# Two more buffers for raw weights, output blocks split ahead, and a dense copy of V in a hybrid S5 and delta-rule layer

## The chip, the core and the metric

The kernel runs on one core of a Trainium2 chip. The metric is the time of one execution in device microseconds. TensorE (PE in the rows) multiplies; its weight loads (PEld) are shown apart. VectorE (DVE), ScalarE (ACT) and GpSimd (POOL) work on tiles in on-chip memory, and SyncE (SP) issues most of the transfers. Smaller is better.

## The reference

One layer of a streaming encoder: 512 tokens of 2048 channels, float32. Cut to what matters here:

```
h  = LN0(x) * (1 + scale_m) + shift_m
p  = h @ W_in                      -> u_ssm, q, k, v, z, beta, a, gate_ssm, gate_gdn
ys = S5 (64 groups x 16 channels, 64 states each) + GLU, then -> 2048
yg = gated DeltaNet (8 heads, chunks of 64), then -> 2048
m  = sigmoid(gate_ssm) * ys + sigmoid(gate_gdn) * yg
x  = LN1(alpha * x + gate_m * (m @ w_mix_out))
h  = LN0(x) * (1 + scale_f) + shift_f
x  = LN2(alpha * x + gate_f * SwiGLU(h))        # hidden size 5632, 44 tiles of 128
```

The scales, shifts and gates come from a small product of the conditioning vector (adaLN).

## The kernel before

**Weights.** Weights are float32 and TensorE multiplies in a reduced float32 type (fp32r), so each weight block is split in two halves. `Weights` does it for a list of blocks of 128x1024 that is planned beforehand in the order of use. SP loads a block of 512 KB into a buffer `raw` (NB = 3 buffers), ACT casts it to `whi`, DVE subtracts and gets `wlo`. A product of one 128-row slice is three matmuls: hi with the activation's hi, lo with it, hi with the activation's lo. `next` hands out the next block. `run_ahead` splits two blocks beyond the one in use. `poll` is asked after every product and issues the next raw load once the planner's clock has passed the last use of the buffer that the load will take.

**Order.** The program is written through a small planner, `Order`: each call of an engine is recorded with a modelled cost, and side lines of work (the S5 mixer, the delta rule, the layer norms) are generators that the planner resumes between the weight products. `yield X` in such a line means: go on when X is ready by the planner's clock. All engine calls have the one line L170, matmuls L211, transposes L216, so groups are told apart by the tiles' names.

**S5.** The 64 groups are done in eight batches (`s5_batch`). Each computes powers V (tile s_V, on GpSimd), transposes them into G, and multiplies them by C into a convolution kernel Kc: two halves of four matmuls in float32, one for each lag tau. The stationary operand of a matmul is a slice of V whose elements lie eight apart. A matmul of this kind leaves two records in the trace.

**End of the mixers.** `switch()` closes the mixers' buffer pools and opens the buffers of the second half. The product with w_mix_out (tiles pm, blocks raw<-in_w_mix_out_dram) follows the merge.

**FFN.** The 44 hidden tiles come in groups of 8, 8, 8, 8, 8 and 4. A tile takes two products (gate and value) and leaves gs, which is split into hi and lo. After a group its part of the output is added to x (`xa`). The last group is different: after its four tiles, 16 output products of 12 matmuls follow, for token tiles t=0 to 3 and in each for column quarters q=0 to 3, each with its residual add and the statistics of LN2. Their eight weight blocks (two for each q) are multiplied by the row gate_f before they are split. Of these, blocks 0 to 2 go through `next` and are split in the usual way, blocks 3 to 7 through `raw_next`: loaded, and scaled and split by the side line `last_parts` just before use. `ws.limit` keeps `run_ahead` from splitting these five.

Of the kernel before, what the change touches and what calls it, by code (L numbers as in the profile page):

```python
# [11 lines left out]
F32 = mybir.dt.float32  # L12
# [146 lines left out]
class Engine:  # L159
# [5 lines left out]
    def __getattr__(self, name):  # L165
        f = getattr(self.e, name)

        def call(*a, **kw):
            assert self.k != "p" or name != "scalar_tensor_tensor"
            r = f(*a, **kw)  # L170
            out = kw.get("out", a[0] if a else None)
            ins = [x for x in _aps(kw, a) if x is not out]
            k = self.k
            if name == "dma_start":
                self.o.run(k, 1.0 if k == "p" else 0.06, out, ins, 0.05 + out.nbytes() / 345e3)
                return r
            n = 1
            for d in out.shape[1:]:
                n *= d
            if name == "bn_stats":  # L180
                n = 512
            if k == "v":
                us = 0.2 + n * (0.00055 if name in ("tensor_scalar", "tensor_copy", "memset") else 0.00105)
            elif k == "a":
                us = 0.2 + n * 0.00086
            elif kw.get("op") is ALU.pow:
                us = 0.2 + 0.17 * n
            else:
                us = 0.2 + n * (0.0021 if name == "tensor_tensor" else 0.0030)
            self.o.run(k, us, out, ins)  # L190
            return r
        return call
# [198 lines left out]
def s5_batch(k, j, prm, d_col):  # L391
# [56 lines left out]
    for half in range(2):  # L448
        pg = k.psum("s5")
        for i in range(4):  # L450
            pe.transpose(pg[:, 128 * i:128 * i + 128], V[:, 4 * half + i].rearrange("p h s -> p (h s)"), k.c(C_ID))
        act.copy(G[:, 4 * half:4 * half + 4].rearrange("p t n -> p (t n)"), pg)
    Kc = k.sm5.tile([128, 15, 16], F32, name="s5Kc", tag="s5Kc")
    pool.memset(Kc[:, 0:7], 0.0)
    for half in range(2):
        pk = k.psum("s5")
        for i in range(4):
            tau = 4 * half + i
            pe.matmul(pk[:, 128 * i:128 * i + 128], lhsT=V[:, :, :, 7 - tau].rearrange("p g h -> p (g h)"),
                      rhs=cf[:, 0, :], start=True, stop=True)  # L460
        yield pk
        pk4 = pk.rearrange("p (t n) -> p t n", t=4)
        v.tensor_tensor(out=pk4, in0=pk4, in1=bc(k.c(C_BD).unsqueeze(1), [128, 4, 128]), op=M)
        v.tensor_reduce(out=Kc[:, 7 + 4 * half:11 + 4 * half], in_=pk.rearrange("p (t g h) -> p t h g", t=4, g=8),
                        axis=mybir.AxisListType.X, op=A)
# [459 lines left out]
NHALF = 8  # L925


GATES_BEFORE = (0, 1, 1, 1, 1, 1, 1, 1)
WB = 1024
NB = 3  # L930


class Weights:


    def __init__(self, k, pool):
        self.k, self.pool = k, pool
        self.specs, self.raw, self.parts, self.names = [], {}, {}, {}
        self.used = self.loaded = self.cut = 0
        self.limit = None  # L940

    def plan(self, src, kts, cols, scale=None):
# [3 lines left out]
    def load(self, upto):  # L946
        while self.loaded < min(upto, len(self.specs)):
            src, kts, cols, _ = self.specs[self.loaded]
            t = self.pool.tile([128, WB], F32, name="raw", tag="raw")
            self.k.sync.dma_start(out=t[:, 0:kts * cols].rearrange("p (k n) -> p k n", k=kts),  # L950
                                  in_=src.rearrange("(k p) n -> p k n", p=128))
            self.raw[self.loaded] = t
            self.names[self.loaded] = t.name
            self.loaded += 1

    def split(self, upto):
        while self.cut < min(upto, len(self.specs) if self.limit is None else self.limit):
            i = self.cut
            self.load(i + 1)
            _, kts, cols, scale = self.specs[i]  # L960
            n = kts * cols
            raw = self.raw.pop(i)
            if scale is not None:
                self.scaled(raw, kts, cols, scale)
            hi = self.pool.tile([128, WB], F32R, name="whi", tag="whi")
            lo = self.pool.tile([128, WB], F32R, name="wlo", tag="wlo")
            self.k.act.copy(hi[:, 0:n], raw[:, 0:n])
            self.k.v.tensor_tensor(out=lo[:, 0:n], in0=raw[:, 0:n], in1=hi[:, 0:n].bitcast(F32), op=S)
            self.parts[i] = tuple(t[:, 0:n].rearrange("p (k n) -> p k n", k=kts) for t in (hi, lo))
            self.cut += 1  # L970
# [28 lines left out]
    def poll(self):  # L999

        i = self.loaded
        if i < len(self.specs) and i < self.cut + NB:
            o = self.k.o
            if i < NB or o.last.get(self.names[i - NB], 0.0) <= o.clock:
                self.load(i + 1)


# [1 line left out]
def kernel(ctx, tc, x, c, w_ada, b_ada, w_in, lam_re, lam_im, log_dt, b_re, b_im, c_re, c_im,  # L1009
# [5 lines left out]
    k = Ctx()  # L1015
# [67 lines left out]
    for hf in range(2):  # L1083
        for q in range(4):
            for c0 in range(0, 16, 2):
                ws.plan(w_mix[0, 128 * c0:128 * c0 + 256, 512 * q:512 * q + 512], 2, 512)
    groups = [(j0, min(HG, NHT - j0)) for j0 in range(0, NHT, HG)]
    ffn_order = []
    for gi, (j0, ng) in enumerate(groups):
        nh = min(NHALF, ng) if gi == 0 else 0  # L1090
        ffn_order.append([(j, [hf]) for hf in range(2) for j in range(nh)] + [(j, [0, 1]) for j in range(nh, ng)])
        for j, _ in ffn_order[-1]:
            for base in (0, HID):
                plan1(f_in[0, :, base + 128 * (j0 + j):base + 128 * (j0 + j) + 128])
        for q in range(4):
            for c0 in range(0, ng, 2):
                r0 = 128 * (j0 + c0)
                ws.plan(f_out[0, r0:r0 + 256, 512 * q:512 * q + 512], 2, 512, q if gi == len(groups) - 1 else None)
    ws.limit = len(ws.specs) - 5


    cst = cpool.tile([128, 128], F32, name="cst")
# [381 lines left out]
    def switch():  # L1484

        o.drain(s5l)
        o.drain(gl)
        o.MARGIN = 0.4
        sps.close()
        gps.close()  # L1490
        per5s.close()
        bp = ctx.enter_context(pool_of(name="bp", bufs=32))
        q2 = ctx.enter_context(pool_of(name="q2", bufs=2))
        P2.extend((bp, q2))

        def operands():
            for dst, src in ((zs, k.dz), (ygs, k.dy)):
                r = load2(src[0])
                for j in range(8):
                    yield r  # L1500
                    nxt = load2(src[j + 1]) if j < 7 else None
                    hi, lo = bt(), bt()
                    if dst is zs:
                        act.copy(nat(hi), by_pos(r))
                        v.tensor_tensor(out=nat(lo), in0=by_pos(r), in1=nat(hi).bitcast(F32), op=S)
                    else:
                        split(hi, lo, r)
                    dst.append((hi, lo))
                    r = nxt
        k.ada_deep = True  # L1510
        o.add(operands())
        o.add(ada_rest())
# [252 lines left out]

    for gi, (j0, ng) in enumerate(groups):
        if gi == len(groups) - 1:
            k.gf_rows = [row_to(t2("ld"), drow[5], q) for q in range(2)]
        for j, hs in ffn_order[gi]:
            if 1 in hs and gi == 0 and j == 0:  # L1770
                o.drain(lnl)
            ffn_tile(gsp[j], hs)
        if gi == len(groups) - 1:
            break
        for q in range(4):
            pss = [k.psum("fo") for _ in range(4)]
            o.until(lambda: k.ada_done)
            gf = row_of(drow[5], q)
            for c0 in range(0, ng, 2):
                hi, lo = ws.next(2, 512)  # L1780
                for t in range(4):
                    prod(pss[t], gsp, t, c0, ng, [hi[:, i, :] for i in range(2)], [lo[:, i, :] for i in range(2)])
                    if c0 + 2 == ng:
                        scaled(t, q, pss[t], gf)


    k.gf_rows += [row_to(bt(F32), drow[5], q) for q in range(2, 4)]
    parts = []

    def last_parts():  # L1790
        for q in range(4):
            his, los = [], []
            if q > 1:
                yield k.gf_rows[q]
            for c0 in range(0, ng, 2):
                if 2 * q + c0 // 2 < 3:
                    hi, lo = ws.next(2, 512)
                    his += [hi[:, i, :] for i in range(2)]
                    los += [lo[:, i, :] for i in range(2)]
                    continue  # L1800
# [58 lines left out]
```

## Time and profile before

| | |
|---|---|
| median of 3 runs | 3115.47 us (3112.6 to 3117.87) |
| profiled execution | 3112.85 us, its span 3111.1 us |
| mean granted TensorE clock | 0.987 |
| PE busy | 97% of the span |
| PEld, DVE, ACT, POOL busy | 80%, 53%, 31%, 26% |
| instructions | 40284 |

The profiled execution's time is that of the whole launch, the span that of its instructions. Busy times are shares of the span over all stages, which differ; what one stage is limited by is seen in the stretches below.

### The profile page before, as it was taken

To read this page: it belongs to the slowest core of one execution; us is meant where nothing else is said; L and a number is where in the kernel's file an instruction comes from. 1 tells how busy PE (TensorE), PEld (TensorE's weight loads), DVE (VectorE), ACT (ScalarE), POOL (GpSimd) and SP (SyncE) were. 2 spreads that over 40 slices of the span, in tenths; PEclk is the share of its full clock that TensorE was granted. 3 is DMA by queue.
4 is the path that set the end of the run, shared out by engine and by line. 5 is a ranking of instruction groups with operands and counts; after the bars stand their busy time and mean duration, and the time that the engine had idled before them with its cause. 6 is when DMAs were issued, how large, how long until landed. Compare 5 with 4: busy or idle time off the path is not lost.

```text
span 3111.1 us, 40284 instructions
## 1 busy us (share of the span) xinstructions
PE 3005.1 (97%) x15953; PEld 2488.9 (80%) x15953; DVE 1650.4 (53%) x2217; ACT 954.8 (31%) x1378; POOL 810.8 (26%) x904
## 2 busy tenths in 40 slices
PE   5999999999999999999899999999999999999996
PEld 3677788888788888888779988888888888888885
DVE  6646666667754577756787543333333333333337
ACT  3333233323332444323355522221221222222121
POOL 2079365555621255200132011003002001200302
PEclk8999999999999999999999999999999999999998
DMA  9743343333333698756776643333333333333342
GB/s 339 263 133 109 97 114 106 100 101 105 95 114 111 211 313 272 243 188 227 256 250 181 178 144 109 95 96 114 95 95 106 105 95 101 109 95 96 110 131 86
DMA packets 508925, 458.14 MB, mean 147 GB/s; under 512 B 56144, under 2 KB 403632, under 8 KB 508736
## 3 DMA queue, kind: packets, MB, share of 16 engines
q1 hardware_dynamic: 485536, 390.03, 41.1%
q0 software_dynamic: 16000, 52.44, 5.2%
q10 hardware_dynamic: 7200, 13.10, 1.2%
q8 instruction: 125, 2.05, 0.3%
q14 instruction: 64, 0.52, 0.1%
HBM read 435.60 MB, written 19.89 MB: 146 GB/s over the span
## 4 chain that ended last, share of the span: by engine, by line
PE 66%; DVE 4%; DMA 3%; issue 2%; ACT 1%; POOL 1%; ACTq 0%; DVEq 0%; SPq 0%; POOLq 0%
PE pm L211 48%; PE px_fo L211 14%; DMA raw<-in_w_mix_out_dram 2%; PE px_gd L211 1%; DVE at L170 1%; DVE wlo L170 1%; ACT whi L170 1%; PE px_s L211 1%; DMA raw<-in_ffn_w_in_dram 1%; DVE aacc L170 0%; DVE st L170 0%; PE px_ada L211 0%; DVE pm L170 0%; DVE raw L170 0%; POOL g_T L170 0%
## 5 line engine op out<-in xcount | busy, mean ns | idle before, releaser
L211 PE MATMUL pm<-at,whi 128*128 128x512 f32 (+1 forms) x3744 | 1133.8, 386 | 0.1
L170 DVE TENSOR_TENSOR wlo<-raw,whi 128x1024 fp32r<-128x1024 f32 x541 | 690.1, 1277 | 819.7 <-ACT whi L170 816.6
L170 ACT CAST whi<-raw 128x1024 fp32r<-128x1024 f32 x541 | 567.2, 1050 | 1061.8 <-PE pm L211 461.4
L211 PEld LDWEIGHTS pm<-at,whi 128*128 128x128 f32 x3744 | 679.4, 189 | 129.4 <-issue 3.5
L211 PE MATMUL pm<-at,wlo 128*128 128x512 f32 (+1 forms) x1872 | 713.0, 381 | 0.0
L211 PE MATMUL pm<-bt,whi 128*128 128x512 f32 (+1 forms) x2464 | 679.7, 362 | 0.0
L211 PEld LDWEIGHTS pm<-bt,whi 128*128 128x128 f32 x2464 | 442.4, 189 | 71.3 <-ACT whi L170 0.5
L211 PE MATMUL pm<-bt,wlo 128*128 128x512 f32 (+1 forms) x1232 | 445.9, 362 | 1.7 <-DVE wlo L170 1.7
L211 PEld LDWEIGHTS pm<-at,wlo 128*128 128x128 f32 x1872 | 353.9, 189 | 68.4 <-DVE wlo L170 0.4
L170 POOL TENSOR_TENSOR at<-at,ld 128x512 f32<-128x512 f32 x80 | 120.4, 1531 | 1003.0 <-DVE ld L170 1003.0
L211 PE MATMUL px_fo<-whi,bt 128*128 128x512 f32 x960 | 298.8, 389 | 0.0
L211 PEld LDWEIGHTS pm<-bt,wlo 128*128 128x128 f32 x1232 | 232.8, 189 | 38.1 <-DVE wlo L170 2.3
L211 PEld LDWEIGHTS px_fo<-whi,bt 128*128 128x128 f32 x960 | 180.1, 188 | 37.4
L211 PE MATMUL px_fo<-wlo,bt 128*128 128x512 f32 x480 | 186.7, 389 | 0.0
L170 DVE SCALAR_TENSOR_TENSOR aacc<-w,ccol,aacc 128x512 f32<-128x512 f32 x180 | 154.4, 858 | 4.5 <-DMA w<-in_w_ada_dram 3.4
L211 PE MATMUL pm<-whi,bt 128*128 128x512 f32 x336 | 109.2, 396 | 8.0 <-DVE at L170 8.0
L211 PE MATMUL px_fo<-whi,at 128*128 128x512 f32 x336 | 108.1, 391 | 1.7 <-ACT whi L170 1.7
L211 PEld LDWEIGHTS px_fo<-wlo,bt 128*128 128x128 f32 x480 | 90.1, 188 | 18.8
L170 DVE SCALAR_TENSOR_TENSOR gs<-gg,pm 128x512 f32<-128x512 f32 x36 | 24.8, 688 | 142.1 <-ACT gg L170 142.1
L170 DVE TENSOR_TENSOR gs<-gs,pm 128x512 f32<-128x512 f32 x36 | 24.7, 687 | 119.6 <-PE pm L211 119.6
L211 PEld LDWEIGHTS pm<-whi,bt 128*128 128x128 f32 x336 | 63.9, 190 | 23.5 <-DVE at L170 10.2
L211 PEld LDWEIGHTS px_fo<-whi,at 128*128 128x128 f32 x336 | 63.5, 189 | 15.2 <-ACT whi L170 2.1
(421 smaller groups left out, 3190.3 us busy)
## 6 DMA issues: line engine op xcount, KB each, us to landing
raw<-in_ffn_w_in_dram SPq DMA_DIRECT2D x208, 512.0 KB
raw<-in_w_in_dram SPq DMA_DIRECT2D x146, 512.0 KB
raw<-in_ffn_w_out_dram SPq DMA_DIRECT2D x88, 512.0 KB
wad<-in_w_ada_dram SPq DMA_DIRECT2D x64, 512.0 KB
w<-in_w_ada_dram SPq DMA_DIRECT2D x128, 256.0 KB
raw<-in_w_mix_out_dram SPq DMA_DIRECT2D x64, 512.0 KB
w<-in_w_ada_dram POOLq DMA_DIRECT2D x96, 256.0 KB, 4.9
gg<-in_w_ada_dram POOLq DMA_DIRECT2D x32, 256.0 KB, 5.2
```

The costliest lines, as they stand in the source:

```text
L170: r = f(*a, **kw)
L211: r = self.e.matmul(out, **kw)
```

## The change

Three parts:

1. In `s5_batch`, ACT copies V into a dense tile Vs, one plane of 128x128 for each lag, and the eight matmuls of the kernel Kc take their stationary operand from there. The tile takes the buffer "K" that later holds another matrix of the batch. ACT's modelled cost for operands of more than three dimensions is raised.
2. From `switch()` on, two more raw buffers (pool "more") stand in a ring with the three of before: raw, more, raw, more, raw. `poll` may then load up to five blocks beyond the last one split.
3. Four of the last eight output blocks (q=0 and q=1) are planned earlier: two behind the last group's first tile and two behind its second. They are loaded there, scaled and split into buffers that are free by then (`kept`, `spare`). Of the four others, two go through `next` and two through `raw_next`, and `ws.limit` leaves the last two out instead of five.

```diff
@@ Engine: modelled cost on ACT
-                us = 0.2 + n * 0.00086
+                us = 0.2 + n * (0.00195 if len(out.shape) > 3 or (ins and len(ins[0].shape) > 3) else 0.00086)
@@ s5_batch
+    Vs = k.t5w("K")
+    act.copy(Vs.rearrange("p (s n) -> p s n", s=8), V.rearrange("p g h s -> p s (g h)"))
+    yield Vs
...
-            pe.matmul(pk[:, 128 * i:128 * i + 128], lhsT=V[:, :, :, 7 - tau].rearrange("p g h -> p (g h)"),
+            pe.matmul(pk[:, 128 * i:128 * i + 128], lhsT=Vs[:, 128 * (7 - tau):128 * (8 - tau)],
                       rhs=cf[:, 0, :], start=True, stop=True)
@@ constants
+EARLY = 4
+MORE = 2
@@ Weights.load
-            t = self.pool.tile([128, WB], F32, name="raw", tag="raw")
+            pool, tag = self.ring[0]
+            self.ring.append(self.ring.pop(0))
+            t = pool.tile([128, WB], F32, name="raw", tag=tag)
+            self.past[tag].append(t.name)
@@ Weights.split
+            if i in self.kept:
+                pairs = self.kept[i]()
+                for s, (hi, lo) in enumerate(pairs):
+                    r = raw[:, cols * s:cols * s + cols]
+                    self.k.act.copy(hi, r)
+                    self.k.v.tensor_tensor(out=lo, in0=r, in1=hi.bitcast(F32), op=S)
+                self.parts[i] = tuple(zip(*pairs))
+                self.cut += 1
+                continue
@@ Weights.poll
-        if i < len(self.specs) and i < self.cut + NB:
-            o = self.k.o
-            if i < NB or o.last.get(self.names[i - NB], 0.0) <= o.clock:
+        tag = self.ring[0][1]
+        n = MORE if tag == "more" else NB
+        if i < len(self.specs) and i < self.cut + (NB + MORE if len(self.ring) > 1 else NB):
+            o, past = self.k.o, self.past[tag]
+            if len(past) < n or o.last.get(past[-n], 0.0) <= o.clock:
                 self.load(i + 1)
@@ the list of blocks
+            if last and j < EARLY // 2:
+                kept += range(len(ws.specs), len(ws.specs) + 2)
+                plan_out(2, True)
+        plan_out(len(out_blocks), last)
-    ws.limit = len(ws.specs) - 5
+    ws.limit = len(ws.specs) - 2
@@ switch
+        more = ctx.enter_context(pool_of(name="more", bufs=MORE))
+        ws.ring = [(wpool, "raw"), (more, "more"), (wpool, "raw"), (more, "more"), (wpool, "raw")]
@@ the last group
+            spare = gsp[ng:] + [[adp.tile([128, 512], F32R, name="w1", tag="w1", bufs=4) for _ in range(2)] for _ in range(2)]
...
+            if gi == len(groups) - 1 and j < EARLY // 2:
+                early += [ws.next(2, 512) for _ in range(2)]
...
@@ last_parts
-                if 2 * q + c0 // 2 < 3:
+                n = 2 * q + c0 // 2
+                if n < EARLY:
+                    his += early[n][0]
+                    los += early[n][1]
+                    continue
+                if n < 6:
```

Where instructions stand now, at three places. On ACT in the first S5 batch (s_G is G, s_K the buffer of the copy of V, g_ the delta rule, go and dg_101 a gate on its way to DRAM, s_S the batch's states):

```order
 L170 COPY s_G<-px_s_2476 128x512
 L170 COPY s_G<-px_s_2482 128x512
+L170 COPY s_K<-s_V 128x1024
 L170 COPY g_MT<-px_gd 128x512
-L170 COPY s_S<-px_s_2571 64x256 x4
 L170 ACTIVATE go<-pm 128x512
 L170 DMA dg_101<-go 128x512
```

The copy of V stands between the copies of G and a copy of the delta rule, and the batch's states are copied later.

On ACT at the first two tiles of the last FFN group, before (whi<-raw are weight blocks, gg the gate's activation, at<-gs the cast of a finished tile):

```order
L170 CAST whi<-raw 128x1024 x18
L170 ACTIVATE gg<-pm 128x512
L170 CAST whi<-raw 128x1024 x2
L170 CAST at<-gs 128x512
L170 CAST whi<-raw 128x1024 x2
L170 ACTIVATE gg<-pm 128x512
```

And there now (bt, w and aacc are the buffers that keep the early output blocks):

```order
L170 CAST whi<-raw 128x1024 x18
L170 ACTIVATE gg<-pm 128x512
L170 CAST bt<-raw 128x512 x4
L170 CAST at<-gs 128x512
L170 CAST whi<-raw 128x1024 x4
L170 ACTIVATE gg<-pm 128x512
L170 CAST w_22922<-raw 128x512
L170 CAST w_22924<-raw 128x512
L170 CAST aacc<-raw 128x512
L170 CAST aacc_22928<-raw 128x512
L170 CAST at<-gs 128x512
L170 CAST whi<-raw 128x1024 x4
```

Where two casts of the next tile's weights stood ahead of the cast of the finished tile, four casts of early output blocks stand now, and the next tile's casts come behind.

On DVE at the first of the last output products, before (raw<-raw,bt scales a block, bt<-raw,bt are its two subtractions, at<-at,pm and at<-at,px_fo residual adds, st statistics):

```order
L170 TENSOR_TENSOR at<-at,pm 128x512
L170 BN_STATS st<-at 128x6
L170 TENSOR_TENSOR raw<-raw,bt 128x1024
L170 TENSOR_TENSOR bt<-raw,bt 128x512 x2
L170 TENSOR_TENSOR raw<-raw,bt 128x1024
L170 TENSOR_TENSOR bt<-raw,bt 128x512 x2
L170 TENSOR_TENSOR raw<-raw,bt 128x1024
L170 TENSOR_TENSOR bt<-raw,bt 128x512 x2
L170 TENSOR_TENSOR raw<-raw,bt 128x1024
L170 TENSOR_TENSOR bt<-raw,bt 128x512 x2
L170 TENSOR_TENSOR at<-at,px_fo 128x512
L170 BN_STATS st<-at 128x6
```

And there now:

```order
L170 TENSOR_TENSOR gs<-gs,pm 128x512
L170 TENSOR_TENSOR bt<-gs,bt 128x512
L170 TENSOR_TENSOR raw<-raw,bt 128x1024
L170 TENSOR_TENSOR bt<-raw,bt 128x512 x2
L170 TENSOR_TENSOR raw<-raw,bt 128x1024
L170 TENSOR_TENSOR bt<-raw,bt 128x512 x2
L170 TENSOR_TENSOR at<-at,pm 128x512
L170 BN_STATS st<-at 128x6
L170 TENSOR_TENSOR at<-at,px_fo 128x512
L170 BN_STATS st<-at 128x6
```

Two blocks are split between the last tile and the first residual add, and none between the residual adds.

## Rows read from the trace of the kernel before

**Rows 1.** The page, busy time, share of the span and instructions of each engine.

```profile
PE 3005.1 (97%) x15953; PEld 2488.9 (80%) x15953; DVE 1650.4 (53%) x2217; ACT 954.8 (31%) x1378; POOL 810.8 (26%) x904
```

**Rows 2.** Stretches: length, busy time by engine (records), TensorE's clock, DMA share, GB/s.

```profile
300.00:900.00 600.00, 577.43 (x4211) 484.12 (x4209) 400.44 (x703) 202.29 (x400) 309.61 (x289) 0.98 0.37 103
1400.00:1440.00 40.00, 40.00 (x178) 33.13 (x177) 25.57 (x30) 13.59 (x15) 0.00 (x0) 1.00 0.61 201
1440.00:1480.00 40.00, 39.70 (x172) 31.85 (x171) 27.84 (x35) 14.95 (x16) 3.24 (x6) 1.00 0.79 254
1480.00:1520.00 40.00, 34.81 (x143) 27.23 (x142) 25.57 (x30) 12.54 (x13) 3.77 (x7) 0.96 0.80 262
1520.00:1560.00 40.00, 36.92 (x149) 28.48 (x148) 33.95 (x49) 15.21 (x16) 12.53 (x16) 0.96 0.76 245
1560.00:1600.00 40.00, 35.15 (x157) 27.57 (x156) 33.63 (x47) 19.91 (x27) 14.73 (x14) 1.00 0.75 247
```

**Rows 3.** Time line of PE at the end: start, duration, first matmuls of t=0, 1, 2.

```profile
3037.03 0.39 PE L211 MATMUL pm<-whi,at 128*128 128x512 f32 x1
...
3060.43 0.39 PE L211 MATMUL pm<-whi,at 128*128 128x512 f32 x1
...
3071.31 0.39 PE L211 MATMUL pm<-whi,at 128*128 128x512 f32 x1
```

**Rows 4.** Groups by form, PE: count, busy us, mean ns, idle before.

```profile
L211 PE MATMUL px_s<-s5Cs,s_V 128*128 128x128 f32 x128 | 32.8, 404 | 0.0
...
L211 PE MATMUL px_gd<-g_k 128*128 128x128 f32 x64 | 8.4, 275 | 0.0
```

**Rows 5.** Groups by form, weight loads of the same matmuls.

```profile
L211 PEld LDWEIGHTS px_s<-s5Cs,s_V 128*128 128x128 f32 x128 | 31.7, 332 | 0.4
...
L211 PEld LDWEIGHTS px_gd<-g_k 128*128 128x128 f32 x64 | 8.2, 191 | 0.5
```

**Rows 6.** Groups by form, ACT: the copy that is already made in each batch.

```profile
L170 ACT COPY s_K<-s_R 128x1024 f32<-128x1024 f32 x8 | 17.6, 2198 | 0.0
```

**Rows 7.** The chain in 1440 to 1600: start, duration, what; three of nine loads.

```profile
1495.94 10.53 DMA raw<-in_w_mix_out_dram
...
1522.82 6.05 DMA raw<-in_w_mix_out_dram
...
1586.29 3.78 DMA raw<-in_w_mix_out_dram
```

**Rows 8.** Waits of PE and ACT in 1440 to 1600: total us, times, longest.

```profile
PE pm L211 <- DVE at L170: 8.0, 5, 2.5
...
ACT whi L170 <- DMA raw<-in_w_mix_out_dram: 56.9, 28, 8.9
```

**Rows 9.** Two stretches of 3.4 us beside a gap; columns as in rows 2.

```profile
1540.60:1544.00 3.40, 0.93 (x5) 0.43 (x4) 3.29 (x6) 1.76 (x2) 1.68 (x3) 1.00 0.96 324
1544.00:1547.40 3.40, 3.40 (x8) 2.72 (x9) 3.33 (x6) 0.47 (x1) 3.32 (x4) 0.50 0.51 178
```

**Rows 10.** Time line of DVE in the last products.

```profile
3053.42 1.22 DVE L170 TENSOR_TENSOR raw<-raw,bt 128x1024 f32<-128x1024 f32 x1
...
3059.65 0.68 DVE L170 TENSOR_TENSOR at<-at,px_fo 128x512 f32<-128x512 f32 x1
...
3095.58 0.68 DVE L170 TENSOR_TENSOR at<-at,px_fo 128x512 f32<-128x512 f32 x1
```

**Rows 11.** Time line of DVE and ACT at a tile's end in the last group.

```profile
3015.47 0.69 DVE L170 TENSOR_TENSOR gs<-gs,pm 128x512 f32<-128x512 f32 x1 [3.35 <-PE pm L211]
...
3016.72 1.05 ACT L170 CAST whi<-raw 128x1024 fp32r<-128x1024 f32 x1
...
3017.80 1.22 DVE L170 TENSOR_TENSOR wlo<-raw,whi 128x1024 fp32r<-128x1024 f32 x1 [0.26 <-ACT whi L170]
```

**Rows 12.** Two more stretches; columns as in rows 2.

```profile
2950.00:3037.00 87.00, 87.00 (x385) 72.07 (x384) 29.58 (x29) 20.46 (x23) 10.11 (x15) 1.00 0.45 130
3060.40:3093.20 32.80, 32.80 (x145) 26.84 (x143) 29.56 (x49) 4.57 (x6) 14.43 (x11) 1.00 0.20 72
```

More of the change, by code (lines that the diff above doesn't have):

```diff
@@ L937, in __init__ @@
         self.k, self.pool = k, pool
-        self.specs, self.raw, self.parts, self.names = [], {}, {}, {}
+        self.specs, self.raw, self.parts, self.kept = [], {}, {}, {}
         self.used = self.loaded = self.cut = 0
+        self.ring, self.past = [(pool, "raw")], {"raw": [], "more": []}
         self.limit = None
@@ L952, in load @@
             self.raw[self.loaded] = t
-            self.names[self.loaded] = t.name
             self.loaded += 1
@@ L1086 @@
                 ws.plan(w_mix[0, 128 * c0:128 * c0 + 256, 512 * q:512 * q + 512], 2, 512)
+    kept = []
     groups = [(j0, min(HG, NHT - j0)) for j0 in range(0, NHT, HG)]
@@ L1091, with plan_out @@
         ffn_order.append([(j, [hf]) for hf in range(2) for j in range(nh)] + [(j, [0, 1]) for j in range(nh, ng)])
+        out_blocks = [(q, c0) for q in range(4) for c0 in range(0, ng, 2)]
+        def plan_out(n, scale=None):
+            for q, c0 in itertools.islice(out_blocks, n):
+                r0 = 128 * (j0 + c0)
+                ws.plan(f_out[0, r0:r0 + 256, 512 * q:512 * q + 512], 2, 512, q if scale else None)
+            del out_blocks[:n]
+        last = gi == len(groups) - 1
         for j, _ in ffn_order[-1]:
@@ L1094 @@
                 plan1(f_in[0, :, base + 128 * (j0 + j):base + 128 * (j0 + j) + 128])
[L1095 to L1098, printed above, removed]
-    ws.limit = len(ws.specs) - 5
+            if last and j < EARLY // 2:
[3 more added lines that the diff above has]
+    ws.limit = len(ws.specs) - 2
     cst = cpool.tile([128, 128], F32, name="cst")
@@ L1767 @@
         if gi == len(groups) - 1:
-            k.gf_rows = [row_to(t2("ld"), drow[5], q) for q in range(2)]
+            q2 = P2[1]
+            k.gf_rows = [row_to(t, drow[5], q) for q, t in enumerate((t2("ld"), t2("ld"), t2("grow")))]
+            spare = gsp[ng:] + [[adp.tile([128, 512], F32R, name="w1", tag="w1", bufs=4) for _ in range(2)] for _ in range(2)]
+            spare += [[adp.tile([128, 512], F32R, name=n, tag=n, bufs=1) for n in ("aacc", "go")],
+                      [q2.tile([128, 512], F32R, name=n, tag=n, bufs=1) for n in ("aacc2", "keep")]]
+            for n, i in enumerate(kept):
+                ws.kept[i] = lambda n=n: spare[2 * n:2 * n + 2]
+            early = []
         for j, hs in ffn_order[gi]:
@@ L1784 @@
                         scaled(t, q, pss[t], gf)
-    k.gf_rows += [row_to(bt(F32), drow[5], q) for q in range(2, 4)]
+    k.gf_rows.append(row_to(bt(F32), drow[5], 3))
     parts = []
@@ L1792, in last_parts @@
             his, los = [], []
-            if q > 1:
-                yield k.gf_rows[q]
+            yield k.gf_rows[q]
             for c0 in range(0, ng, 2):
-                if 2 * q + c0 // 2 < 3:
+                n = 2 * q + c0 // 2
[4 more added lines that the diff above has]
+                if n < 6:
                     hi, lo = ws.next(2, 512)
```

## The prediction

> **What bounds the kernel now.** I read the page first, then stretches. TensorE is busy 97% of the span [rows 1], so a gain must shorten TensorE's own work or fill one of its few gaps. A busy TensorE is not a full one, so I counted matmul records in stretches of equal length instead of trusting the busy time. At full rate, in 1400 to 1440, TensorE finishes 178 records in 40 us, one per 0.225 us; in the four stretches of 40 us behind it, the product with the mixers' output weights, it finishes 172, 143, 149 and 157 [rows 2]. That product loses time although its busy column hardly falls. The other stretch I looked for is the S5 and delta-rule phase, 300 to 900: busy 577.43 of 600, so 22.6 us idle there [rows 2]. The third is the end, where the output products of four token tiles t=0 to 3 follow one another. Tile t=0 starts at 3037.03, t=1 at 3060.43, t=2 at 3071.31: 23.4 us for the first and 10.88 for the next, with the same 48 accumulations each [rows 3].
>
> Each of the three parts of the change falls on one of these places.
>
> **(a) The dense copy of V.** It removes nothing and replaces 64 strided stationary operands by dense ones, for eight ACT copies. Records in the view by form: 128 matmul records with a column of V as stationary operand take 32.8 us, in 16 groups (two per batch), so 2.05 us a group of eight records. The delta rule's products of the same shape and type, 128x128x128 float32 with a dense operand, take 8.4 us for 64, 1.05 us for eight [rows 4]. The only difference that the rows offer is the read of the stationary operand: its weight load takes 332 ns against 191 [rows 5]. So a group gets 1.0 us shorter, 16 in all.
>
> Here a page speaks against the change. The Trainium skill, "TensorE: Matmul & The Clock Gate", section "LDWEIGHTS (loading the stationary operand)", gives a load as columns divided by 1.2 GHz and says that only the columns matter; by it a dense operand would save nothing and the sum would lose these 16 us. The measured loads differ by 1.7 times at the same 128 columns, so the row decides here.
>
> The price is eight ACT copies with the same strided read. The same copy of another matrix in each batch, s_K<-s_R, takes 2198 ns [rows 6], so 17.6 us of ACT. ACT is busy 202.29 of 600 us there [rows 2]: at the low end this is hidden beside other work, at the high end each copy stands in front of what the K products need and all 17.6 is paid. Only a S5 batch waits for its own copy, and TensorE has weight products to run meanwhile, so I take 2. (a) = −16 + 2 = **−14**, bounds −17 and +1.6.
>
> **(b) Two more raw buffers.** They remove the rule that a load can only start when the third block before it is used up. In the four stretches, 4×178 = 712 records would have been done at full rate; 172+143+149+157 = 621 were. The 91 missing are worth 91×0.225 = 20.5 us. How fast must a transfer be? A block is 12 matmuls, 12×0.225 = 2.7 us. With three buffers a buffer comes round every 8.1 us, of which the cast takes 1.05 and the subtraction 1.22 [rows 11], so 5.8 us are left for the load. With five it is 13.5 − 2.3 = 11.2. The chain of that stretch holds nine pieces of these loads, from 3.78 to 10.53 us, the middle one 6.05 [rows 7]. So half the pieces are too slow for three buffers, and all fit five. ACT's casts waited 56.9 us for these loads [rows 8]. The mean of the DMA engines is 0.75 to 0.80 busy [rows 2], so there is a reserve in rate, but not a big one: loads that start earlier compete with operands' loads. TensorE also waited 8.0 us for DVE, which draining products holds up [rows 8]; that the buffers do not mend. Part of the lost time is the clock: after a gap (TensorE busy 0.93 of 3.4 us) the next 3.4 us ran at 0.50, the lower level (1.2 GHz), with 8 records in place of 15 [rows 9]; without the gap this is not paid. I take three quarters of 20.5: **−15**, bounds −6 (the waits for DVE stay, and the gaps move) and −21 (all).
>
> A page would say that the loads were fast enough before. The Trainium skill, "DMA: Bandwidth & Descriptors", section "Anatomy of one DMA — SWDGE (gpsimd) path", fits a transfer as 2.0 us plus bytes over 436 GB/s; from it I estimate 3.2 us for 512 KB, and with that (b) would be near 0. The loads here come from another queue and share the engines, and the fastest piece of the chain is 3.78.
>
> **(c) Four output blocks split early.** Moved: blocks 4 to 7 of the eight (2 per quarter q). Before, five blocks are split just before use, each one DVE scaling, two ACT casts and two DVE subtractions; the scalings of two neighbours start at 3053.42 and, two blocks later, the residual add of q=1 in t=0 at 3059.65, so 3.1 us of DVE a block [rows 10]. TensorE waits for that in t=0: 23.4 against 10.88, so 12.5 us [rows 3]. After, four blocks are already split and two remain, 6.2 us of DVE beside 10.88 us of products. Can DVE then keep up? The last residual add of all (t=3, q=3) starts at 3095.58, 35.9 us behind that one [rows 10], and DVE is busy 29.56 of 32.8 us in that stretch [rows 12]. Counted from the first product: the last tile's gated product and its subtraction about 2.2, two splits 6.2, the add of q=0 with its statistics about 1.3, then the 35.9 from q=1's add on: 45.6 us. TensorE's side puts the same add at 58.55 (3037.03 to 3095.58) − 12.5 = 46.05. So DVE just follows: −12.5.
>
> The price lies earlier. In the order after, ACT splits the early blocks when tiles 0 and 1 of the last hidden group are planned, and the next tile's first weight cast then stands behind the cast of that tile's gated product, which waits for the tile's last matmul; before, two weight casts stood ahead of it. Queued behind it is the split that TensorE needs next. Its length is read from a tile's end: product at 3015.47, its cast, a weight cast at 3016.72 of 1.05, its subtraction at 3017.80 of 1.22, over at 3019.02: 3.55 us, of which some 0.25 is covered by matmuls that need the cast alone, so 3.3 [rows 11]. Such a gap brought the lower clock in [rows 9], which cost 7 records, 1.6 us, there; I add 1. Two places: 2×4.3 = +8.6. The lower end is 0, if the next blocks are cast before by other casts still in hand; the upper is 2×(3.55+1.6) = 10.3, with 2 more if the 12.4 us of DVE for the early blocks don't quite fit beside the tiles' matmuls, where DVE was busy 29.58 of 87 us [rows 12]. (c) = −12.5 + 8.6 = **−4**, bounds −12.5 and 0.
>
> **(d) The order of the mixers moves** (the copies change the planner's clocks; the S5 batches are spread a little later). 22.6 us are idle there before [rows 2]; I take 0, and ±6 as a bound: a quarter of that idle either way.
>
> **Sum.** −14 −15 −4 = −33 on the profiled 3112.85 us: 3080. The median of the runs is 2.6 us above that one, so **3082**. With every better bound met it would be 3059, with every worse one (+1.6 −6 +0 +6) 3117; its own range goes halfway to each, 3070 to 3100. A time within 0.2% (6.2 us) of before cannot be told from no change.
>
> **Rivals.**
> 1. *The w_mix product does not speed up* (DVE's draining and the shared DMA engines set it): for it speak the 8.0 us of waits for DVE [rows 8] and the DMA share of 0.75 to 0.80 [rows 2]; against it, the 56.9 us that ACT waited for loads [rows 8]. (b) shrinks to −3: 3094. The page's rule on transfers would lead there too.
> 2. *The dense operand brings nothing*, because products hide the longer weight load, and the copies cost 2: (a) = +2, so 3098. Against it, the matmul records are themselves further apart [rows 4]. This is where the page's rule on weight loads leads.
> 3. *The bubbles at the tile ends cost more than the tail gives*: (c) = +4, so 3090.
> 4. *Slower*: each 2.2 us copy waits on ACT for V, which GpSimd computes, and the delta rule's copies behind it wait too. If every one of the eight batches loses 5 us so, 40 in all, the gains are gone: 3122 us; it decides from 33 us on, 4.1 a batch. For it speaks the order, where the copy now stands ahead of the delta rule's copy g_MT; against it, that ACT is busy only a third of that time [rows 2].
>
> **How the numbers follow.** The sum 0.66, rival 1 0.13, rival 2 0.07, rival 3 0.06, rival 4 0.08, half of which still lies within 0.2% of before and half beyond. That is 0.92 faster, 0.04 the same, 0.04 slower. The range from 3062, near where all better bounds meet, to 3100 holds the first four cases almost whole and leaves out rival 4.
>
> **What the profile after would show.** (a) Products with V's copy at about 1.05 us per eight records, and eight copies near 2.2 us. (b) Some 170 records or more per 40 us in the product with the mixers' output weights, and few waits of weight casts for loads; if records stay near 150 there, rival 1 holds. (c) t=0's products in about 11 us, and two gaps of 3 us at the ends of tiles 0 and 1 of the last group; if there are none, (c) is −12. (d) Idle time of 300 to 900 near 22; at 55 or more, rival 4 holds. I am wrong if the copies of V hold ACT's queue, or the early loads slow one another.

## The result and the profile after

The changed kernel takes 3074.47 us (median of 4 runs, 3071.26 to 3076.15) against 3115.81 us (median of 4) before: a ratio of 0.9871, 95% interval 0.9859 to 0.9882, 41 us less. Its profiled execution took 3075.24 us, its span is 3073.5 us, 37.6 less than the one before.

Where these 37.6 us came from is read stage by stage. Both kernels do the same weight products in the same order, so the n-th record on the tiles pm and px_fo is the same product in both, and a stage is the time from its first product to the next stage's first.

| stage | before | after | difference |
|---|---|---|---|
| mixers, from the first product (67.56; 66.20) to the first with w_mix_out (1420.30; 1394.39) | 1352.7 | 1328.2 | −24.6 |
| product with w_mix_out, to the first FFN tile (1622.62; 1582.83) | 202.3 | 188.4 | −13.9 |
| FFN, first halves of eight tiles, to 1726.29; 1690.72 | 103.7 | 107.9 | +4.2 |
| second halves, to the first output product (1818.45; 1784.02) | 92.2 | 93.3 | +1.1 |
| FFN, to 2862.95; 2828.53 | 1044.5 | 1044.5 | 0.0 |
| a group's output and the last group's tiles, to t=0's first product (3037.03; 3011.14) | 174.1 | 182.6 | +8.5 |
| last products, to the last group of records (3092.85; 3054.82) | 55.8 | 43.7 | −12.1 |

The rest lies at the two ends: the first product comes 1.4 us earlier, and what follows the last records takes 0.4 us more.

The stretches of the changed kernel, columns as in rows 2: the mixers, the steady rate, three stretches of 40 us in the product with w_mix_out, and 50 us before and at the last group's first tiles.

```profile
300.00:900.00 600.00, 587.16 (x4393) 488.02 (x4392) 419.45 (x726) 228.89 (x431) 317.22 (x300) 1.00 0.39 109
1380.00:1420.00 40.00, 40.00 (x178) 33.09 (x177) 26.56 (x32) 13.55 (x14) 0.44 (x1) 1.00 0.68 222
1420.00:1460.00 40.00, 40.00 (x175) 32.43 (x175) 27.91 (x33) 15.52 (x16) 2.81 (x6) 1.00 0.83 264
1460.00:1500.00 40.00, 40.00 (x177) 32.85 (x176) 33.36 (x44) 15.39 (x15) 8.49 (x12) 1.00 0.91 312
1500.00:1540.00 40.00, 34.93 (x150) 27.57 (x149) 37.76 (x51) 15.74 (x17) 16.22 (x16) 1.00 0.76 241
2880.00:2930.00 50.00, 50.00 (x222) 41.42 (x221) 17.25 (x20) 9.92 (x11) 14.11 (x12) 1.00 0.40 116
2930.00:2980.00 50.00, 44.19 (x185) 35.18 (x184) 21.94 (x25) 14.65 (x20) 0.00 (x0) 0.97 0.43 127
```

The w_mix_out product now runs at 175 and 177 records per 40 us, near the steady 178, where [rows 2] has 172 and 143; the DMA share rose to 0.91. One stretch still falls to 150. In the mixers 12.8 us are idle in place of 22.6, and the granted clock is 1.00 in place of 0.98. At 2930 to 2980, 185 records stand where 222 would: 37 × 0.225 = 8.3 us lost, new in this kernel.

Groups by form of the changed kernel: the products with the copy of V, their weight loads, and the copy itself.

```profile
L211 PE MATMUL px_s<-s5Cs,s_K 128*128 128x128 f32 x128 | 17.4, 279 | 1.5 <-ACT s_K L170 1.3
...
L211 PEld LDWEIGHTS px_s<-s5Cs,s_K 128*128 128x128 f32 x128 | 16.3, 191 | 3.1 <-ACT s_K L170 2.1
...
L170 ACT COPY s_K<-s_V 128x1024 f32<-128x1024 f32 x8 | 17.4, 2174 | 0.0
```

The products went from 32.8 to 17.4 us [rows 4], a weight load from 332 to 191 ns [rows 5], and TensorE waited 1.3 us for a copy.

Waits of the changed kernel, ACT in 1415 to 1575 (first row) and PE in 1600 to 1700 (second): us in total, times, longest.

```profile
ACT whi L170 <- DMA raw<-in_w_mix_out_dram: 4.3, 2, 3.3
```

```profile
PE px_tr L216 <- ACT ld L170: 6.8, 4, 4.4
```

Two more rows of waits: PE of the changed kernel in 1415 to 1575 (first), and PE of the kernel before in 1620 to 1735, where its layer norm's transposes stand (second).

```profile
PE pm L211 <- DVE at L170: 4.9, 3, 3.3
```

```profile
PE px_tr L216 <- ACT ld L170: 2.3, 2, 2.1
```

ACT's casts waited 4.3 us for those loads, where they had waited 56.9 [rows 8]. TensorE's wait for DVE is still 4.9 us, where it was 8.0 [rows 8]. The row on px_tr is where some of the gain was given back: TensorE waits 6.8 us, 2.3 before, for the tiles ld of the second layer norm, whose transposes px_tr stand in front of the second halves of the FFN tiles.

Time line of PE in the changed kernel, the two gaps at tile ends and the first products of t=0 and t=1.

```profile
2939.87 0.73 PE L211 MATMUL pm<-bt,whi 128*128 128x512 f32 x2 [2.38 <-ACT whi L170]
2941.13 0.50 PE L211 MATMUL pm<-bt,wlo 128*128 128x512 f32 x1 [0.53 <-DVE wlo L170]
...
2965.13 0.73 PE L211 MATMUL pm<-bt,whi 128*128 128x512 f32 x2 [2.38 <-ACT whi L170]
2966.39 0.80 PE L211 MATMUL pm<-bt,wlo 128*128 128x512 f32 x1 [0.53 <-DVE wlo L170]
...
3011.14 1.52 PE L211 MATMUL pm<-bt,at 128*128 128x512 f32 x6
...
3022.10 1.52 PE L211 MATMUL pm<-bt,at 128*128 128x512 f32 x6
```

The two gaps stand where the prediction put them, 2.38 + 0.53 = 2.9 us each, and t=0 takes 10.96 us in place of 23.4 [rows 3]. The granted clock behind them is not the same twice. Here are some 4 us behind the first gap and behind the second:

```profile
2941.10:2945.00 3.90, 3.87 (x17) 3.20 (x18) 2.24 (x2) 0.61 (x1) 0.00 (x0) 1.00 0.67 200
2966.40:2970.40 4.00, 4.00 (x11) 3.19 (x12) 2.21 (x2) 0.57 (x1) 0.00 (x0) 0.58 0.67 189
```

Counted by products, the first tile end lost 3.5 us at full clock, and the second 5.0, with 11 records in 4.0 us where 18 fit.

### The profile page after: what moved, and what is told of

The parts are those of the page before. It is cut to its first block, busy times and chain, and to the rows that moved or that the text cites. A ratio compares the mean times of both kernels' runs of the same rounds, so it can differ in the third digit from the quotient of the medians.

```text
span 3073.5 us, 40281 instructions
## 1 busy us (share of the span) xinstructions
PE 2979.1 (97%) x15953; PEld 2467.8 (80%) x15953; DVE 1652.6 (54%) x2218; ACT 973.8 (32%) x1387; POOL 816.6 (27%) x904
## 5 line engine op out<-in xcount | busy, mean ns | idle before, releaser
L211 PE MATMUL px_fo<-whi,at 128*128 128x512 f32 x320 | 101.8, 389 | 0.0
L170 ACT CAST bt<-gs 128x512 fp32r<-128x512 f32 x36 | 22.4, 621 | 167.9 <-DVE gs L170 167.9
```

The source lines that it names most:

```text
L211: r = self.e.matmul(out, **kw)
```

## The experiments

Twelve kernels, each timed against the kernel before on one chip. Median us, that of before in the same comparison, ratio with interval, and the difference to before of the stages above in the profiled execution (mixers; w_mix_out; both FFN halves; last tiles; last products):

| kernel | us | before | ratio | mixers | w_mix | halves | tiles | last |
|---|---|---|---|---|---|---|---|---|
| dense_alone | 3088.18 | 3114.63 | 0.9912 (0.9898 to 0.9926) | −22.6 | +1.7 | −0.7 | 0.0 | 0.0 |
| copy_unread | 3096.63 | 3114.63 | 0.9943 (0.993 to 0.9956) | −12.6 | +5.0 | −3.1 | 0.0 | 0.0 |
| cost_alone | 3105.82 | 3113.87 | 0.9972 (0.9962 to 0.9982) | −13.8 | +4.9 | +2.9 | 0.0 | 0.0 |
| more_alone | 3103.65 | 3114.63 | 0.9966 (0.9954 to 0.9978) | +7.0 | −12.6 | +1.7 | 0.0 | 0.0 |
| early_alone | 3112.71 | 3114.63 | 0.9994 (0.9985 to 1.0003) | −2.9 | −0.9 | +0.5 | +9.8 | −12.1 |
| early_first | 3066.55 | 3113.87 | 0.9855 (0.9841 to 0.9869) | −29.8 | −12.4 | +5.4 | 0.0 | −12.1 |
| ln_on_dve | 3075.27 | 3113.87 | 0.9878 (0.9865 to 0.9891) | −26.5 | −12.7 | +4.8 | +9.4 | −12.1 |
| first_and_ln | 3066.42 | 3113.87 | 0.9849 (0.9835 to 0.9863) | −21.5 | −12.3 | +2.6 | 0.0 | −12.1 |
| ln_margin0 | 3069.92 | 3112.55 | 0.9863 (0.9849 to 0.9876) | −27.5 | −12.4 | +9.2 | 0.0 | −12.1 |
| ln_margin_neg | 3059.34 | 3112.55 | 0.9831 (0.9818 to 0.9844) | −28.3 | −13.9 | −1.9 | 0.0 | −12.1 |
| copy_twice | 3096.99 | 3112.55 | 0.9953 (0.994 to 0.9965) | +9.3 | −12.6 | +4.4 | 0.0 | −12.1 |
| copy_uncounted | 3081.49 | 3115.19 | 0.9896 (0.9879 to 0.9913) | −13.5 | −12.5 | +5.3 | 0.0 | −12.1 |

How far one profile's mixers can be trusted is seen in the five kernels early_first to ln_margin_neg, whose mixers have the changed kernel's instructions in the same order: −21.5 to −29.8. Their product with w_mix_out and their last products agree within 1.6 and 0.1 us. A profile is one execution, and some lie off their kernel's median: those of copy_unread, more_alone and copy_twice 4.3 to 4.6 us above it, those of early_alone and ln_margin_neg 3.8 and 4.0 below. A difference of that size in one kernel's mixers is therefore not read, such as the +7.0 of more_alone.

**The three parts alone**

dense_alone: before, with the diff's lines for ACT's cost, the copy and the products, and nothing else.

> Before, with the dense copy of V and ACT's new modelled cost alone. Theory (the 25.9 us gained by the end of the mixers belong to this part: 15.4 us of the products with V, some 10 us of order and clock that come with it): 26 us less than before, about 3090. Rival (the 10 us beyond the products are chance of the order in the changed kernel): 14 to 16 us less, about 3100. By both the product with w_mix_out and the tail stay as before.

Measured: 26.4 us less, as the theory had it. But the whole is not the dense read, as the next two show.

copy_unread: the same without the products' line.

```diff
+    Vs = k.t5w("K")
+    act.copy(Vs.rearrange("p (s n) -> p s n", s=8), V.rearrange("p g h s -> p s (g h)"))
+    yield Vs
...
             pe.matmul(pk[:, 128 * i:128 * i + 128], lhsT=V[:, :, :, 7 - tau].rearrange("p g h -> p (g h)"),
```

> Before, with the eight copies of V and the new modelled cost, but the products still read V itself, so the copy is made for nothing. Theory (the dense read pays, the copies are hidden): within 5 us of before, 3113 to 3120, the products at 32.8 us for 128 records. Rival 1 (the copies cost what ACT spends on them): 17 us more, 3133. Rival 2 (what the mixers gained beyond the products is order): 10 us less, 3106.

Measured: 18.0 us less, with the products as slow as before. The theory fell, and so did rival 1; rival 2 had the sign and about half the size. Groups by form of this kernel:

```profile
L211 PE MATMUL px_s<-s5Cs,s_V 128*128 128x128 f32 x128 | 32.2, 394 | 0.0
```

So a copy that nobody reads makes the kernel faster. Reading it adds 3096.63 − 3088.18 = 8.4 us by the medians, of the 15 that the records get shorter. With five runs each, spread over 10 to 13 us, that size is rough; in the profiles the mixers of the two kernels, which have the same order, differ by 10.0. The rest of dense_alone's gain stands in the stretch 300 to 960, here of before, copy_unread and the next kernel, cost_alone:

```profile
300.00:960.00 660.00, 637.43 (x4593) 533.76 (x4592) 433.73 (x762) 222.73 (x446) 328.37 (x308) 0.98 0.37 104
```

```profile
300.00:960.00 660.00, 649.69 (x4750) 543.44 (x4750) 447.79 (x777) 242.92 (x460) 327.96 (x308) 1.00 0.38 108
```

```profile
300.00:960.00 660.00, 654.16 (x4789) 547.91 (x4788) 439.97 (x777) 227.86 (x451) 322.69 (x308) 1.00 0.39 108
```

Idle time of TensorE is 22.6, 10.3 and 5.8 us, and the clock is 0.98, 1.00 and 1.00.

cost_alone: before, with only the first line of the diff, by which the planner counts another copy at 2.2 us. No instruction is added or removed.

> Before, with ACT's new modelled cost alone: no copy, no dense read; the planner only counts the copy s_K<-s_R at 2.2 us in place of 1.1 and orders the mixers by that. Theory (the 18 us of the unread copy come from the order, which the modelled cost alone brings about): 12 to 18 us less than before, about 3100. Rival (the copy itself, with its wait for the tile, spaces the lines so; the modelled cost alone does nothing): within 4 us of before, about 3114.

Measured: 8.0 us less, between the two; in the profile the mixers are 13.8 shorter, and some of it is lost again in the stages behind. The same instructions in another order are worth that much.

more_alone: before, with the ring of five raw buffers alone.

> Before, with the two more raw buffers alone. Theory (15 us gained in the product with w_mix_out and 7 in the first half tiles behind it, then 12 paid at the second layer norm's transposes, which are late next): 8 to 10 us less, about 3106. Rival (that wait is due to the mixers' other order and not to these buffers): 20 us less, about 3096.

Measured: 11.0 us less; the stage of w_mix_out is 12.6 shorter, and in the four kernels of the table without the ring it is between 0.9 shorter and 5.0 longer. The size is near the theory's, but not its second half: the halves of the FFN tiles lose only 1.7 here, so the wait for the layer norm isn't this part's own.

early_alone: the changed kernel with V read directly, the old cost and three raw buffers; only the early output blocks are left of the change.

> Before, with the four output blocks split early alone. Theory (12 us gained in the last products, 8.5 paid in two gaps at the ends of the last group's first two tiles): 3 to 4 us less, about 3112. Rival (the gaps come only where five raw buffers have moved the splits): 12 us less, about 3104.

Measured: 1.9 us less, within the uncertainty; in the profile 9.8 us lost at the tiles and 12.1 gained at the end. The gaps belong to this part; here the granted clock fell behind both of them, to 0.67 and 0.58 over 4 us, which makes the loss 9.8 and not 8.5. The three medians add up to 26.4 + 11.0 + 1.9 = 39.3 of the 41 us.

**The gaps at the tile ends**

early_first: the early output blocks and the next tile's first two blocks are both split ahead of the finished tile's gated product.

```diff
+        if early is not None:
+            early += [ws.next(2, 512) for _ in range(2)]
+            ws.run_ahead()
         v.tensor_tensor(out=gg, in0=gg, in1=pss[1][:, sl], op=M)
```

> The changed kernel, with the early output blocks and the next tile's first two blocks both split ahead of the finished tile's gated product (two whi casts stand ahead of the cast of gs again, as before the change). Theory (those two gaps are the 8.5 us lost in the last group): 8 to 9 us less than the changed kernel, about 3066, and no gap of 3 us at 2930 to 2980. Rival (the four early blocks cost ACT and DVE time that TensorE waits for, wherever they stand): within 3 us of 3074.

Measured: 3066.55, 7.9 less than the changed kernel's median (6.0 when each is set against the kernel before in its own comparison). Its stretch at those tiles:

```profile
2920.00:2970.00 50.00, 50.00 (x222) 41.39 (x222) 24.87 (x28) 16.66 (x23) 0.00 (x0) 1.00 0.53 155
```

222 records in 50 us: no gap, and the stage's loss is 0.0. The same DVE and ACT work for the early blocks is hidden there; only its place cost time.

**The second layer norm**

ln_on_dve: the changed kernel, with the affine step on DVE for the second half.

```diff
-                affine(r, st1[ti], lg, lb, 0 if ti == 1 or q == 0 else 2)
+                affine(r, st1[ti], lg, lb, 0 if ti == 1 or q == 0 or hf == 1 else 2)
```

> The changed kernel, with the affine step of the second half's first layer norm as two DVE instructions for all eight tiles, where two of them were so and six were one ACT and two GpSimd instructions. Theory (that layer norm is late next behind the faster product with w_mix_out, and TensorE waits for its transposes): the line ends sooner, and 6 to 12 us go, about 3066. Rival (what TensorE waits for is the planner's place of the last transposes, however fast the line is; or DVE, which has the weights' subtractions too, becomes the limit): within 3 us of 3074 or above.

> The changed kernel with both edits (the next tile's blocks split first; the second half's layer norm on DVE). Theory: the two gains lie at different places and add, about 3057. Rival (only the gaps at the tile ends go): about 3066.

Measured: 3075.27 and, with early_first's edit, 3066.42, both without a gain beyond that edit. The speed of the layer norm's instructions is not what TensorE waits for. (The 12 us that the expectations speak of were counted from the middle of the stage; over both halves it is 5.3.) What differs is where the transposes stand. Of the 32, before has eight groups of four among the products; in the changed kernel, three of the groups stand together behind the last product of the first halves, with nothing to cover them. Time line of PE at the end of the first halves, before and in the changed kernel:

```profile
1725.14 0.60 PE L216 MATMUL px_tr<-cst,ld 128*128 128x128 f32 x4
1725.50 0.48 PE L211 MATMUL pm<-bt,whi 128*128 128x256 f32 x2
```

```profile
1683.63 0.60 PE L216 MATMUL px_tr<-cst,ld 128*128 128x128 f32 x4
1688.61 0.47 PE L216 MATMUL px_tr<-cst,ld 128*128 128x128 f32 x1 [4.38 <-ACT ld L170]
1689.32 1.75 PE L216 MATMUL px_tr<-cst,ld 128*128 128x128 f32 x7 [0.23 <-ACT ld L170]
1690.72 0.78 PE L211 MATMUL pm<-bt,whi 128*128 128x256 f32 x2
```

In cost_alone, which has three raw buffers, the three groups stand together too; more_alone, dense_alone and copy_unread have them as before. So it is the order again, and not the faster w_mix_out product by itself.

ln_margin0 and ln_margin_neg: early_first, with the planner's lag changed while that norm's line runs.

```diff
     lnl = o.add(ln_half(1))
+    o.MARGIN = 0.0
...
                 o.drain(lnl)
+                o.MARGIN = 0.4
```

> The kernel early_first, with the planner's lag for side lines (MARGIN, by which a line's step is held back after its data are ready in the plan) at 0 in place of 0.4 while the second half's layer norm runs. Theory (twelve of that norm's 32 transposes stand together behind the last tile of the first half because its line is just longer than its cover; with a shorter lag they stand among the products again): the 12 us given back there go, 3055 to 3060. Rival (steps recorded so early are not ready on the chip, and TensorE waits for them among the products): 3064 to 3070.

> As the one before, with the lag at -1.0: steps are recorded up to 1 us before their data are ready in the plan. Theory: the line ends sooner yet, but single steps come too early, 3055 to 3062. Rival: TensorE waits at most of the eight groups of transposes, above 3064.

Measured: 3069.92 with 0.0, 3.4 above early_first, which alone is hardly more than the spread of the runs, though the two halves are 3.8 longer in the profile; and 3059.34 with −1.0, 7.2 better. PE's waits in 1600 to 1700, of the first and of the second:

```profile
PE px_tr L216 <- ACT ld L170: 9.1, 6, 4.2
```

```profile
PE px_tr L216 <- ACT ld L170: 2.1, 3, 1.3
```

With 0.0 the theory fell: the groups stand among the products, but in pairs close together, and TensorE waits for them six times: the rival's case. With −1.0 the line starts some 140 records earlier, the groups are spread, and the stage is 1.9 us shorter than before the change. The place decides; the lag is only a way to move it, and not a steady one. This is the fastest kernel of the study.

**What a copy costs**

copy_twice: early_first with the copying line written twice. copy_uncounted: the second one is issued past the planner.

```diff
     act.copy(Vs.rearrange("p (s n) -> p s n", s=8), V.rearrange("p g h s -> p s (g h)"))
+    act.e.copy(Vs.rearrange("p (s n) -> p s n", s=8), V.rearrange("p g h s -> p s (g h)"))
```

> The kernel early_first, with the copy of V made twice in each batch (the second over the first). It prices the copy itself, 17 us of ACT. Theory (ACT has room, the copies are hidden): within 4 us of 3066.5. Rival (each copy is paid where it stands, since the products wait for it): 3080 or more.

> The same instructions as copy_twice, but the planner does not count the second copy, so the order of everything else is that of early_first. Theory (the 30 us of copy_twice came from the order that counting the copy brings about, not from ACT's 17 us): 3066 to 3072. Rival (the copies themselves cost that): 3090 to 3100.

Measured: 3096.99 and 3081.49, against 3066.55 without a second copy. For copy_twice the theory fell; for copy_uncounted neither expectation held, the time lies midway: 15 us for copies that the planner doesn't know, and 15 more, with the same instructions, when it knows them. The planner's figure for a copy of V, whose operands have three dimensions, is 0.2 + 1024 × 0.00086 = 1.08 us, where the chip takes 2.17; the raised cost falls on s_K<-s_R alone. No run counts the copy at its measured time. PE's waits in 300 to 960, first of copy_uncounted, then of copy_twice:

```profile
PE px_s L211 <- ACT s_K L455: 12.7, 8, 3.4
```

```profile
PE px_s L216 <- POOL s_V L170: 9.2, 6, 2.6
PE px_gd L211 <- DVE St L170: 7.8, 3, 3.5
PE px_gd L211 <- DVE g_T L170: 5.2, 5, 1.8
PE px_ada L211 <- DVE aacc L170: 4.6, 1, 4.6
...
PE px_s L211 <- ACT s_K L170: 1.3, 3, 0.5
```

Uncounted, the copy is paid where it is read: eight waits, 12.7 us. Counted, the planner puts the products behind it and that wait is 1.3 us in all, as in the changed kernel; but everything else moves as well, and here it moves badly: TensorE waits for V, for the delta rule's state St and its inverse g_T.

## Why the prediction was right, and where its steps were off

Forecast was 3082 us (range 3062 to 3100), measured 3074.47; the sum of −33 stands against −37.6 in the profiles. The total fits better than its terms, and that is in part luck: the mixers gained 24.6 where (a) had 14, and 5.3 were lost at a layer norm for which no term stood.

**(a) The dense copy.** The products' term was right: 16 forecast, 32.8 − 17.4 = 15.4 measured. The row on the weight load decided rightly: 332 ns became 191. The Trainium skill, "TensorE: Matmul & The Clock Gate", section "LDWEIGHTS (loading the stationary operand)", gives a load by its columns alone; the trace does not agree, with 332 and 191 ns at the same 128 columns. For the copies 2 us were forecast, and TensorE's wait for them is 1.3. That they are cheap goes with the planner counting them, which the prediction did not say: eight second copies that it does not count cost 15. What the term missed is that shorter records don't all come back as time: beside copy_unread, which makes the same copies in the same order, the dense read gave 8.4. Part of the difference is waiting: in 300 to 960 TensorE is idle 13.8 us in dense_alone and 10.3 in copy_unread.

**(b) The buffers.** The mechanism and its size were right: 15 forecast, 13.9 in the stage, and ACT's wait for loads fell from 56.9 to 4.3 us. The pieces of the chain [rows 7] were the right guide. By the fit of the Trainium skill, "DMA: Bandwidth & Descriptors", section "Anatomy of one DMA — SWDGE (gpsimd) path", which is for another queue, three buffers would have done; the 13.9 us gained do not agree. The part that stays is the one named, TensorE's wait for DVE: 4.9 us of it are left, and the stretch with 150 records has DVE busy 37.76 of 40. A term was missing for what lies behind that stage: there the layer norm's transposes take back 5.3 us, and the prediction named no wait. Of the cause it is shown that the place of the transposes in the program decides (ln_margin_neg), and that neither this part alone nor the norm's own speed does.

**(c) The early blocks.** The mechanism was right: the last products gained 12.1 for 12.5, and the two gaps cost 8.5 for 8.6. That the second figure fits so well is luck. The prediction added 1 us for the lower clock to each gap; here the clock fell behind the second alone (0.58, against 1.00 behind the first), so that the two cost 5.0 and 3.5, and in early_alone it fell behind both. early_first shows that the gaps came from the place of these splits in the order, and not from the amount of work.

**(d) The mixers' order.** Mis-sized: 0 with ±6 forecast. The copies with their order, but without the dense read (copy_unread), made the kernel 18.0 us faster where the prediction had +2 for the copies and 0 for the order. Counting one copy differently (cost_alone) shortened the mixers by 13.8 us in the profile and the whole kernel by 8.0 in the median; counting a second copy or not (copy_twice, copy_uncounted), with the same instructions, changed the median by 3096.99 − 3081.49 = 15.5. This is the largest part of what was left over, and the reason why the result lies below the forecast. The bound of a quarter of the idle time had no row behind it; the idle time of 300 to 960 fell from 22.6 to 10.3 (copy_unread) and 5.8 us (cost_alone), and the lower clock in the rows went with it. How a given edit will move this order can't be told from the trace of before. That stays open: the study shows the size of the effect, not a rule for its sign.

Of the rivals, the first (w_mix_out not faster) is excluded by more_alone, the second by the shorter records and by dense_alone beside copy_unread, the third by the stages' −12.1 and +8.5. The fourth, in which the copies hold up the delta rule, didn't occur. Mixers can get longer by counted copies, though: those of copy_twice take 9.3 us more than before the change in spite of the dense read. Its waits are for V and the delta rule, as that rival has it; that the copies' hold on ACT causes them is not shown.

## What to carry to other kernels

Where a planner writes the program's order, an edit has two prices, its own and that of the new order, and the second can be the larger (here 8.4 us from the dense read beside 18.0 that came with the copies and their order); a run with only the planner's number changed, and one with the work issued past it, tell them apart. A stage that was changed is followed to the end of the next one, since a side line that was just covered may stand elsewhere in the new order and stick out (here 5.3 us). Work that is split ahead goes in front of the instruction that waits for the stage's last product, not behind it.

## What the runs showed of the hardware

The same float32 weight load of 128 columns took 332 ns with its elements 32 bytes apart and 191 ns with them side by side, and the products behind it 256 and 136 ns each (32.8 and 17.4 us for 128). A copy of 128x1024 read with that stride took 2174 ns on ACT, a cast of the same size read side by side 1.05 us [rows 11]. Gaps of the same length did not always bring the lower clock: of the two in the changed kernel, 2.38 + 0.53 us each, it followed the second (0.58 over 4.0 us) and not the first (1.00).
